# A two-layer trunk kernel: where the T2 weight sums of one feed-forward product wait for their second use, how its activations are re-read, and how its norm is computed

## The chip, the cores and the metric

The kernel runs on one core of a Trainium2 chip. The metric is the device time of one execution in microseconds. Before the change, three runs took 1405.94, 1411.48 and 1411.53 us, so the median is 1411.48.

The core has a matrix engine (TensorE, PE in the profile, with its weight loads as PEld), a vector engine (VectorE, DVE), a scalar engine (ScalarE, ACT), GpSimd (POOL) and SyncE (SP). The data is in DRAM; engines work on tiles of 128 partitions in SBUF, and TensorE accumulates in PSUM. Every transfer is a DMA that an engine's queue issues; here SyncE, ScalarE and GpSimd issue them. An engine works through its own instructions in order, so an instruction that waits holds back those behind it.

## The reference

A trunk of two layers runs over 256 context tokens and 256 latent tokens, with model width D = 1024 and FFN width F = 2816. The mixer of layer 0 is an mLSTM; that of layer 1 is multi-head latent attention (MLA). Each mixer is followed by a convolutional FFN, and each of the four sub-layers ends in the same norm:

```python
def _conv_ffn(h, w_in, conv_w, conv_b, w_out):
    gate, up = jnp.split(h @ w_in, 2, axis=-1)
    return (jax.nn.silu(_dwconv(gate, conv_w, conv_b)) * up) @ w_out
...
        f = _conv_ffn(_modulate(x, ml[3], ml[4]), ffn_w_in[i], ...)
        x = _layer_norm(ALPHA * x + ml[5] * f, ln_g[i, 1], ln_b[i, 1])
```

`_layer_norm` subtracts the mean of a row of 1024 and divides by the root of its variance plus EPS. In layer 1 the MLA first makes small projections: `w_dkv` (1024 to 256 + 64) of context and latent, `w_dq` (1024 to 384) of the latent, a norm of each, and from those `w_ukv` (keys `kn` and values) and `w_uq` (queries). Context tokens are needed in layer 1 as keys and values only.

The change concerns the second product of layer 0's FFN (activations of 512 tokens times `w_out`, 2816 x 1024), the norm behind it, and the order of MLA's projections.

## The kernel before, in words

**Arithmetic.** All is float32, computed on TensorE with operands of type fp32r split in two parts, hi and lo = value - hi. A product is three matmuls, hi x hi, hi x lo and lo x hi (L382 to L384 in `mm3`, and the loop of L1386). So each weight and each activation is split once: ScalarE casts hi, VectorE subtracts lo.

**The stream of weights.** All weights pass, in one fixed order, through the class `Stream`, in tiles of 128 x 1024 (512 KB; "raw"). `_load` (L271) takes a tile from a ring of buffers and asks for it: a plain load on SyncE (L280) or, for two sorts named below, a re-load from DRAM on SyncE (L277) followed by a GpSimd DMA that adds another weight to the tile in passing (L278). `_split` makes hi and lo (L322 ScalarE, L325 VectorE) in one of three buffers `w` (NB = 3), or, for keys marked wide, in two tiles of the pool `u` (NU = 31 tiles of 128 x 1024). `use(key)` gives the next weight to its product and splits ahead: up to AHEAD = 8 weights, as far as `limit` and the three buffers allow. A raw buffer becomes free with its split, and then the next load is asked for.

**The product of the FFN in question** (`w_fout0`, L1351) uses a scheme with seven block products where plain blocking has eight. Tokens are cut in context and latent, channels in even and odd blocks of 128, columns in halves of 512. Four sums of activations (S1 to S4) and four of weights (T1 to T4) are formed; T4 = T2 + B21. `_sum` (L291 to L293) makes T1, T2 and T3 of three raw tiles on VectorE, SUMS = 5 weights ahead. The weights come as six rounds i = 0..5 of `yt2` (T2), `y11`, `yt3`, `yt1` (24 matmuls of 128x512 each, 12 in round 5), and then in the order YLAST: `y21` of 0, 1, `yt4` of 0 to 5, `y21` of 2 to 5, `y22` of 0 to 5. T2 is used in the first part and needed again for T4 in the second: `_split` stores it to a DRAM tile `t2d` on ScalarE's queue (L324), and the load of `yt4` reads it back and has B21 added. An earlier product of the mLSTM (`vt2`, `vt4`) does the same.

Activations: `act_sums` (L1328) is called while the FFN's first product runs. It makes the operands of the first part in SBUF (`fa`, `fs`), and GpSimd stores those of the second part, named "2", "3" and "S4", to DRAM tiles `fd` (L1340, L1346). `operand()` (L1363) is called after each product from the seventh on: ScalarE's queue re-reads one operand, 128 x 512, as two DMAs of 128 KB (L1367, tile `zr`), and the operand asked for two calls before is split (L1373 ScalarE, L1374 VectorE, tile `fz`). PSUM holds four pairs of sums, p6, p1, p7, p5. Between the parts, ScalarE and VectorE form u1, u2, u3, v of them (L1420 to L1435); TensorE's next `y21` adds into p1 only when the copy of L1420 has read it.

**Rows and norm.** After 14 and 18 products GpSimd asks for the gate rows and the residual rows `z` (L1411, L1415), first latent, then context. `add()` (L1442 to L1444) multiplies the product by the gate, adds it to `z` and takes batch statistics per half row. `z_norm` (L1479) turns them into mean and variance (L1486), takes a root on ScalarE (L1488) and a reciprocal, and normalizes one half of the row on VectorE (L1492) and one on ScalarE (L1493). These pieces are Python generators in a list `bg`; `tick(n)` after a product emits n steps of them. `latent()` runs from the third `y21` on, so that its transposes `zT` (`lat_T`, L1198) fall between the last products; `context()` runs in `mla_down`.

**Layer 1's projections.** `mla_down` (L1590): `dkv` of the latent, whose three weights stay in the three `w` buffers until the context has used them too (`hold`, `unhold`); the context's adds and norm; `dq` (L384); transposes `ckT` (L1550) of the normalized rows `ckr` (L1503), and their split (L1554, L1555); the context's transposes; `ukn(1)` (latent keys); `dkv` of the context. `mla` (L1637): `uv((2,3))` (latent values), transposes `cqT` (L1649), `uqr` (qr), `ckT` of the context, `ukn(0)`, `uv((0,1))` (context keys and values), rotations, then `queries(i)` and the scores.

**Order.** The tile scheduler of the language orders instructions on each engine by its own estimate and by data; `keep_in_program_order` (`pin`) holds single instructions to the order of the program, and inside `manual_schedule` (the second part of the product and `mla_down`) TensorE's order is that of the program.

## Time and profile before

| | before |
|---|---|
| profiled execution, its own time | 1407.69 us |
| its span | 1405.8 us |
| mean granted TensorE clock | 0.992 |
| three runs | 1405.94, 1411.48, 1411.53 us |
| PE busy, 941 to 1030 us (second FFN product) | 72.67 of 89 us |
| PE busy, 1030 to 1120 us (its end, norm, projections) | 82.59 of 90 us |
| PE busy, 1120 to 1406 us | 272.39 of 286 us |

The table's last three rows are from the view that cuts the span in stretches. In the rows below, L12 is line 12 of the kernel before; "out<-in" names the tiles; "x24" is a count; `[10.90 <-ACT u L1420]` is time in which the engine waited for the instruction named. Rows of single instructions begin with the start and the duration in microseconds; where several equal ones are drawn together, the duration covers them all. PEclk is the granted clock of TensorE, 1.00 at full speed. "DMA share" is the mean busy share of the core's 16 DMA engines.

### The profile page before, as it was taken

The page shows a single profiled execution, that of the slowest core. Times are in us where ns is not written, and L with a number is a line of the kernel's source. Part 1 is how long each engine was busy: PE and PEld are TensorE (multiplying, and loading weights), DVE is VectorE, ACT ScalarE, POOL GpSimd, SP SyncE. Part 2 cuts the span into 40 slices and gives each one's busy share as a digit, 9 for nine tenths or more (in the row PEclk, how much of TensorE's full clock was granted, in tenths as well). Part 3 has the DMA queues.
Part 4 walks back from the last instruction along what each step waited for, and adds up shares of the span by engine and source line. Part 5 has one row for each costly group of instructions (what it writes and reads, how often), then busy time and mean ns, then how long its engine had stood idle before and what let it go on. Part 6 is the DMA issues. An engine that isn't in the chain of part 4 may idle for free.

```text
span 1405.8 us, 19141 instructions
## 1 busy us (share of the span) xinstructions
PE 1356.3 (96%) x6903; PEld 1141.3 (81%) x6903; DVE 1068.4 (76%) x1706; ACT 697.7 (50%) x1173; POOL 121.2 (9%) x215
## 2 busy tenths in 40 slices
PE   6999999999999999999999999999698899999997
PEld 3788888888788888878888888888477898899986
DVE  6598756687688697698799887679487788777773
ACT  6585444445544535374553433335356567455560
POOL 0032000011011001110011000000200101000000
PEclk9999999999999999999999999999899999999999
DMA  9689848779666374676857877547976325357750
GB/s 338 220 290 318 287 163 244 242 264 302 214 220 187 115 233 157 201 226 202 256 158 263 273 230 237 169 141 243 300 221 190 125 76 195 127 188 227 207 190 31
DMA packets 97903, 297.63 MB, mean 212 GB/s; under 512 B 12136, under 2 KB 24808, under 8 KB 97808
## 3 DMA queue, kind: packets, MB, share of 16 engines
q1 hardware_dynamic: 68672, 218.52, 48.4%
q0 software_dynamic: 17472, 57.57, 13.1%
q10 hardware_dynamic: 11664, 20.32, 4.0%
q8 instruction: 54, 0.88, 0.3%
q14 instruction: 41, 0.34, 0.1%
HBM read 262.90 MB, written 33.46 MB: 211 GB/s over the span
## 4 chain that ended last, share of the span: by engine, by line
PE 87%; DMA 5%; DVE 4%; ACT 2%; issue 1%; SPq 0%; ACTq 0%; DVEq 0%
PE fin L382 9%; PE fin L383 9%; PE fin L384 9%; PE tok L382 6%; PE tok L383 6%; PE tok L384 6%; PE y L1386 5%; PE qk L382 4%; PE qk L384 4%; PE qk L383 4%; PE y L383 3%; PE y L384 3%; PE y L382 3%; DMA zr<-fd 2%; PE up L382 2%; PE up L384 2%
## 5 line engine op out<-in xcount | busy, mean ns | idle before, releaser
L325 DVE TENSOR_TENSOR w<-raw,w 128x1024 fp32r<-128x1024 f32 (+1 forms) x289 | 347.8, 1206 | 181.1 <-ACT w L322 175.0
L322 ACT CAST w<-raw 128x1024 fp32r<-128x1024 f32 (+1 forms) x289 | 299.5, 1037 | 337.4 <-PE fin L384 105.2
L383 PE MATMUL fin<-h,w 128*128 128x256 f32 (+1 forms) x696 | 231.8, 333 | 0.0
L384 PE MATMUL fin<-h,w 128*128 128x256 f32 (+1 forms) x696 | 231.5, 333 | 0.0
L382 PE MATMUL fin<-h,w 128*128 128x256 f32 (+1 forms) x696 | 231.3, 333 | 0.1
L511 DVE SCALAR_TENSOR_TENSOR junk<-ar,bc 128x1024 f32<-128x1024 f32 x128 | 156.1, 1219 | 4.2 <-ACT bc L553 1.8
L383 PEld LDWEIGHTS fin<-h,w 128*128 128x128 f32 x696 | 132.2, 190 | 13.1 <-DVE h L1211 0.2
L384 PEld LDWEIGHTS fin<-h,w 128*128 128x128 f32 x696 | 132.2, 190 | 12.7
L382 PEld LDWEIGHTS fin<-h,w 128*128 128x128 f32 x696 | 131.9, 190 | 13.1 <-ACT h L1210 0.3
L382 PE MATMUL qk<-xc,w 128*128 128x512 f32 x256 | 100.7, 393 | 0.0
L384 PE MATMUL qk<-xc,w 128*128 128x512 f32 x256 | 100.0, 390 | 0.0
L383 PE MATMUL qk<-xc,w 128*128 128x512 f32 x256 | 99.8, 390 | 0.0
L1386 PE MATMUL y<-w,fz 128*128 128x512 f32 x198 | 48.6, 403 | 13.9 <-ACT u L1420 10.9
L1386 PEld LDWEIGHTS y<-w,fz 128*128 128x128 f32 x198 | 37.6, 193 | 23.6 <-ACT u L1420 11.8
L382 PEld LDWEIGHTS qk<-xc,w 128*128 128x128 f32 x256 | 48.1, 188 | 10.1 <-issue 0.4
L384 PEld LDWEIGHTS qk<-xc,w 128*128 128x128 f32 x256 | 48.1, 188 | 9.9
L383 PEld LDWEIGHTS qk<-xc,w 128*128 128x128 f32 x256 | 48.1, 188 | 9.7
L382 PE MATMUL up<-hT,w 128*128 128x512 f32 x128 | 50.5, 394 | 0.5 <-ACT hT L387 0.5
L383 PE MATMUL up<-hT,w 128*128 128x512 f32 x128 | 50.1, 392 | 0.4 <-DVE hT L388 0.4
L384 PE MATMUL up<-hT,w 128*128 128x512 f32 x128 | 50.1, 392 | 0.3 <-DVE w L388 0.3
L383 PE MATMUL tok<-w,hT 128*128 128x512 f32 x128 | 49.8, 389 | 0.0
L382 PE MATMUL tok<-w,hT 128*128 128x512 f32 x128 | 49.8, 389 | 0.0
(432 smaller groups left out, 2964.1 us busy)
## 6 DMA issues: line engine op xcount, KB each, us to landing
raw<-in_ws SPq DMA_DIRECT2D x287, 512.0 KB, 4.4
ar<-in_adaT SPq DMA_DIRECT2D x80, 512.0 KB, 4.8
adaw<-in_ada_w SPq DMA_DIRECT2D x32, 256.0 KB, 6.0
t2d<-raw ACTq DMA_DIRECT2D x13, 512.0 KB, 4.6
raw<-t2d SPq DMA_DIRECT2D x13, 512.0 KB, 7.6
raw<-in_ws POOLq DMA_DIRECT2D x13, 512.0 KB, 9.2
zr<-fd ACTq DMA_DIRECT2D x33, 128.0 KB, 5.8
xmd<-xr POOLq DMA_DIRECT2D x16, 256.0 KB, 4.7
```

The costliest lines, as they stand in the source:

```text
L322: k.nc.scalar.copy(h[:, :cols], src)
L325: k.nc.vector.tensor_sub(l[:, :cols], src, h[:, :cols])
L382: mm(out, w[0], x[0], start=start, stop=False)
L383: mm(out, w[0], x[1], start=False, stop=False)
L384: mm(out, w[1], x[0], start=False, stop=stop)
L511: nc.vector.scalar_tensor_tensor(o, w, 1.0, self.bc[j], op0=ALU.mult, op1=ALU.mult, accum_out=col[:, k, j:j + 1])
L1386: nc.tensor.matmul(ps[b], a[:, p, ts], w[q][:, cs], start=j == 0 and n == 0 and not more, stop=j == 10 and n == 2, skip_group_check=True)
```

## The change

- **T2 stays in SBUF.** For the FFN's product, T2 lives in a tile of the pool `u` (at most six). When VectorE has subtracted its lo, GpSimd adds B21 to that same tile by one DMA, and `yt4` takes it as its raw tile. The store to `t2d` and the re-load are left out (the mLSTM's product keeps them). The ring of raw buffers loses the two `u` tiles that it had in this stage.
- **Re-reads.** The DRAM tile `fd` holds two neighbouring blocks side by side, so an operand is re-read by one DMA of 256 KB instead of two of 128. `operand()` runs every other product from the twelfth on in the first part, and splits the operand asked for three calls before.
- **Rows.** The gate and `z` rows are asked for at `yt4` of round 0 (latent) and 3 (context).
- **Norm.** `add()` takes the row sum with the addition. `z_norm` gets the variance from two Squares on ScalarE with the mean as bias, and normalizes the whole row on ScalarE. The context's first two adds move to `y22` of rounds 0 and 1, and two steps are emitted after each later `y22`.
- **Splitting ahead.** The `dkv` weights are wide (tiles of `u`, not the three `w` buffers). `limit` is set to the projections' keys at the start of the product, and to the fourth weight of the product before the FFN's first one. The sums of weights are bounded by `limit` too.
- **Order of projections.** `uv((2,3))` moves ahead of `dkv` of the context; `ukn(0)` and `uv((0,1))` move behind `queries(0)` and `queries(1)`.

```diff
@@ -111 +111 @@
-        add(("dkv", 0, c), m * 320)
+        add(("dkv", 0, c), m * 320, True)
@@ -251 +251 @@
-                          [("ar", 2)] * 2 + [("u", NU)] * 2))
+                          [("ar", 2)] * 2))
@@ -255,2 +255,11 @@
-    def ring(self, j):
-        return [x for x in self.bufs if x[0] <= j][-1]
+        self.y0 = keys.index(("yt2", 0, 0))
+        self.slot, self.t2 = [], {}
+        n = {}
+        for j, key in enumerate(keys):
+            j0, ring = [x for x in self.bufs if x[0] <= j][-1]
+            if key[0] in ("yt2", "yt4"):
+                self.slot.append(("t2", NU, 6))
+                continue
+            tag, bufs = ring[n.get(j0, 0) % len(ring)]
+            n[j0] = n.get(j0, 0) + 1
+            self.slot.append((tag, bufs, [x[0] for x in ring].count(tag)))
@@ -265,3 +274,5 @@
-        j0, ring = self.ring(self.nl)
-        tag = ring[(self.nl - j0) % len(ring)][0]
-        return [self.tags[j] for j in self.raw].count(tag) < [x[0] for x in ring].count(tag)
+        key = self.order[self.nl][0]
+        if key[0] == "yt2" and key[2] and self.nu < self.y0 + 4 * max(key[2] - 2, 0):
+            return False
+        tag, _, n = self.slot[self.nl]
+        return [self.tags[j] for j in self.raw].count(tag) < n
@@ -273,5 +284,7 @@
-        j0, ring = self.ring(j)
-        tag, bufs = ring[(j - j0) % len(ring)]
-        t = k.pool.tile([128, CW], F32, tag=tag, name="raw", bufs=bufs)
-        if key[0] in ("vt4", "yt4"):
-            k.nc.sync.dma_start(t[:, :cols], k.t2d[key[0][0], key[1], key[2]][:, :cols])
+        tag, bufs, _ = self.slot[j]
+        if key[0] == "yt4":
+            t = self.t2.pop(key)
+        else:
+            t = k.pool.tile([128, CW], F32, tag="u" if tag == "t2" else tag, name="raw", bufs=bufs)
+        if key[0] == "vt4":
+            k.nc.sync.dma_start(t[:, :cols], k.t2d[key[1], key[2]][:, :cols])
@@ -279 +292 @@
-        elif key[0] not in ("vt2", "yt2"):
+        elif key[0] not in ("vt2", "yt2", "yt4"):
@@ -302 +315 @@
-        while self.nsum < min(j + SUMS, self.n):
+        while self.nsum < min(j + SUMS, max(self.limit, j + 1)):
@@ -323,2 +336,2 @@
-            if key[0] in ("vt2", "yt2"):
-                k.nc.scalar.dma_start(k.t2d[key[0][0], key[1], key[2]][:, :cols], src)
+            if key[0] == "vt2":
+                k.nc.scalar.dma_start(k.t2d[key[1], key[2]][:, :cols], src)
@@ -325,0 +339,4 @@
+            if key[0] == "yt2":
+                t4 = ("yt4",) + key[1:]
+                k.nc.gpsimd.dma_start(src, self.ws[self.ids[t4][0], :, :cols], accum_op=ALU.add)
+                self.t2[t4] = raw
@@ -589,2 +606 @@
-        self.t2d = {(n, p, j): self.dr.tile([128, 1024], F32, name="t2d")
-                    for n, a, b in (("v", 2, 4), ("y", 1, 6)) for p in range(a) for j in range(b)}
+        self.t2d = {(p, j): self.dr.tile([128, 1024], F32, name="t2d") for p in range(2) for j in range(4)}
@@ -1336 +1352,3 @@
-        d = self.dr.tile([128, 768], F32, name="fd")
+        if j % 2 == 0:
+            self.fd.append(self.dr.tile([128, 3, 512], F32, name="fd"))
+        d = self.fd[-1][:, :, j % 2 * 256:j % 2 * 256 + 256]
@@ -1340 +1358 @@
-        nc.gpsimd.dma_start(d[:, 0:512], x2)
+        nc.gpsimd.dma_start(d[:, 0:2], x2.rearrange("p (x n) -> p x n", x=2))
@@ -1346 +1364 @@
-        nc.gpsimd.dma_start(d[:, 512:768], x1[:, a])
+        nc.gpsimd.dma_start(d[:, 2], x1[:, a])
@@ -1349 +1366,0 @@
-        self.fd.append(d)
@@ -1358 +1375 @@
-        off = {"2": 0, "3": 256, "S4": 512}
+        off = {"2": 0, "3": 1, "S4": 2}
@@ -1366,2 +1383,2 @@
-                for h, j in enumerate(js):
-                    pin(nc.scalar.dma_start(r[:, h * 256:(h + 1) * 256], self.fd[j][:, off[x]:off[x] + 256]))
+                n = 256 * len(js)
+                pin(nc.scalar.dma_start(r[:, :n], self.fd[i][:, off[x], :n]))
@@ -1369 +1386 @@
-            if len(got) > 2 or not parts and got:
+            if len(got) > 3 or not parts and got:
@@ -1391,0 +1409,2 @@
+        st.limit = kv0
@@ -1396 +1415 @@
-        z, gate = [None] * 4, []
+        z, gate = [None] * 4, [None, None]
@@ -1406 +1425 @@
-                if n >= 6:
+                if n >= 11 and n % 2:
@@ -1408,8 +1426,0 @@
-                if n in (14, 18):
-                    g = 1 - len(gate)
-                    r = self.uf("gate")
-                    nc.gpsimd.dma_start(r, self.gd[0, 5][1 - g:2 - g, :].to_broadcast([128, 1024]))
-                    gate.append(r)
-                    for b in range(2):
-                        z[2 * g + b] = self.uf("z")
-                        nc.gpsimd.dma_start(z[2 * g + b], x1d[2 * g + b])
@@ -1431,2 +1442 @@
-        gate = gate[::-1]
-        stats = [self.tiny(12, "st").rearrange("p (a b) -> p a b", b=6) for _ in range(4)]
+        sums = [self.tiny(4, "zs") for _ in range(4)]
@@ -1437,0 +1448,8 @@
+        def rows(g):
+            r = self.uf("gate")
+            nc.gpsimd.dma_start(r, self.gd[0, 5][1 - g:2 - g, :].to_broadcast([128, 1024]))
+            gate[g] = r
+            for b in range(2):
+                z[2 * g + b] = self.uf("z")
+                nc.gpsimd.dma_start(z[2 * g + b], x1d[2 * g + b])
@@ -1438,0 +1457 @@
+            i = c.start // 512
@@ -1443,2 +1462,2 @@
-                nc.vector.tensor_tensor(zz, zz, r, op=ALU.add)
-                nc.vector.bn_stats(stats[2 * g + b][:, c.start // 512], zz)
+                nc.vector.scalar_tensor_tensor(zz, zz, 1.0, r, op0=ALU.mult, op1=ALU.add,
+                                               accum_out=sums[2 * g + b][:, i:i + 1])
@@ -1449 +1468 @@
-            for _ in self.z_norm(z[2:4], stats[2:4]):
+            for _ in self.z_norm(z[2:4], sums[2:4]):
@@ -1457 +1476 @@
-            yield from self.z_norm(z[0:2], stats[0:2])
+            yield from self.z_norm(z[0:2], sums[0:2])
@@ -1459 +1477,0 @@
-        st.limit = kv0
@@ -1468 +1486,3 @@
-                if (name, i) == ("yt4", 0):
+                if name == "yt4" and i in (0, 3):
+                    rows(1 if i == 0 else 0)
+                if (name, i) == ("yt4", 3):
@@ -1472 +1492,3 @@
-                self.tick(1)
+                if name == "y22" and i < 2:
+                    next(low)
+                self.tick(2 if name == "y22" and i else 1)
@@ -1475 +1497 @@
-                    self.bg.append(add(0, lo, p1))
+                    low = add(0, lo, p1)
@@ -1481 +1503 @@
-    def z_norm(self, zs, stats):
+    def z_norm(self, zs, sums):
@@ -1484,10 +1506,13 @@
-        for z, st in zip(zs, stats):
-            mv = self.tiny(2, "mv")
-            nc.vector.bn_aggr(mv, st)
-            rs = self.tiny(1, "rs")
-            nc.scalar.activation(rs, mv[:, 1:2], AF.Sqrt, bias=self.keps, scale=1.0)
-            nc.vector.reciprocal(rs, rs)
-            nm = self.tiny(1, "nm")
-            nc.vector.scalar_tensor_tensor(nm, mv[:, 0:1], -1.0, rs, op0=ALU.mult, op1=ALU.mult)
-            nc.vector.tensor_scalar(z[:, 0:512], z[:, 0:512], mv[:, 0:1], rs, op0=ALU.subtract, op1=ALU.mult)
-            nc.scalar.activation(z[:, 512:1024], z[:, 512:1024], AF.Identity, bias=nm, scale=rs)
+        for z, v in zip(zs, sums):
+            nc.vector.tensor_tensor(v[:, 0:1], v[:, 0:1], v[:, 1:2], op=ALU.add)
+            nc.vector.tensor_scalar(v[:, 0:1], v[:, 0:1], -1.0 / D, None, op0=ALU.mult)
+            for h in range(2):
+                jk = self.s2("jk")
+                nc.scalar.activation(jk, z[:, h * 512:(h + 1) * 512], AF.Square, bias=v[:, 0:1], scale=1.0,
+                                     accum_out=v[:, 2 + h:3 + h])
+            yield
+            nc.vector.tensor_tensor(v[:, 2:3], v[:, 2:3], v[:, 3:4], op=ALU.add)
+            nc.scalar.activation(v[:, 2:3], v[:, 2:3], AF.Sqrt, bias=self.keps, scale=1.0 / D)
+            nc.vector.reciprocal(v[:, 2:3], v[:, 2:3])
+            nc.vector.tensor_tensor(v[:, 0:1], v[:, 0:1], v[:, 2:3], op=ALU.mult)
+            nc.scalar.activation(z, z, AF.Identity, bias=v[:, 0:1], scale=v[:, 2:3])
@@ -1625,0 +1651 @@
+        self.uv((2, 3))
@@ -1641 +1666,0 @@
-        self.uv((2, 3))
@@ -1665,3 +1689,0 @@
-        self.ukn(0)
-        self.uv((0, 1))
-        self.ckT = self.wk = self.wv = None
@@ -1763 +1784,0 @@
-        Ps, PTs = {}, {}
@@ -1765,0 +1787,4 @@
+        Ps, PTs = {}, {}
+        self.ukn(0)
+        self.uv((0, 1))
+        self.ckT = self.wk = self.wv = None
@@ -1865,0 +1891 @@
+        st.limit = st.y0 + 4
```

## The prediction

> **What bounds the kernel now.** I read the page's shares first, then a table by stretch, then the waits of the stretch the change touches, then single instructions.
>
> ```profile
> PE 1356.3 (96%) x6903; PEld 1141.3 (81%) x6903; DVE 1068.4 (76%) x1706; ACT 697.7 (50%) x1173; POOL 121.2 (9%) x215
> ```
> ```profile
> core 0: us, PE busy (x) PEld busy (x) DVE busy (x) ACT busy (x) POOL busy (x), PEclk, DMA share, GB/s
> 1005.00:1035.00 30.00, 16.66 (x62) 12.44 (x63) 17.58 (x25) 12.55 (x19) 1.96 (x3) 0.83 0.92 277
> 1035.00:1067.00 32.00, 32.00 (x149) 26.50 (x148) 22.88 (x36) 18.56 (x27) 0.00 (x0) 1.00 0.56 169
> 1067.00:1100.00 33.00, 26.84 (x173) 25.80 (x172) 31.38 (x72) 21.93 (x51) 2.20 (x4) 0.90 0.63 196
> ```
> TensorE is busy 96% of the span, so a change that leaves its 6903 matmuls alone can win only where TensorE waits. The widest hole is 1005 to 1035 (16.66 busy of 30, clock 0.83, DMA engines 92% busy); a smaller one follows at 1067 to 1100. Both lie in the stretch that is edited. What ends the waits there (engine, line, releaser: total, times, longest):
>
> ```profile
> PE y L1386 <- ACT u L1420: 10.9, 1, 10.9
> PE ckT L1550 <- DVE ckr L1503: 5.8, 2, 4.8
> PE y L1386 <- DVE w L325: 2.6, 2, 2.3
> PE y L1386 <- ACT w L322: 2.5, 2, 1.6
> PE kn L383 <- DVE ckT L1555: 2.3, 1, 2.3
> PE kn L382 <- ACT ckT L1554: 0.9, 1, 0.9
> PE qr L382 <- ACT cqT L1649: 0.4, 1, 0.4
> ```
> ScalarE's queue just before the 10.9:
>
> ```profile
> 1007.02 1.04 ACT L322 CAST w<-raw 128x1024 fp32r<-128x1024 f32 x1 [4.25 <-DMA zr<-fd]
> ...
> 1014.23 0.62 ACT L1373 CAST fz<-zr 128x512 fp32r<-128x512 f32 x1 [5.34 <-DMA zr<-fd]
> ...
> 1014.75 0.58 ACT L1420 COPY u<-y 128x512 f32<-128x512 f32 x1
> ```
> The copy that frees TensorE's accumulator (L1420) is ready at 1004 but stands in ScalarE's queue behind two casts that wait for re-read activations (zr). Those land late because the queues carry this, all at once (last two numbers: KB each, median us to landing):
>
> ```profile
> zr<-fd ACTq DMA_DIRECT2D x33, 128.0 KB, 5.8
> raw<-t2d SPq DMA_DIRECT2D x5, 512.0 KB, 10.6
> raw<-in_ws POOLq DMA_DIRECT2D x5, 512.0 KB, 14.4
> z<-x1d POOLq DMA_DIRECT2D x4, 512.0 KB, 14.0
> ```
> ```profile
> DMA to landing us min/median/max: 2.5/5.8/19.3
> ```
> The last row is zr's alone: worst 19.3 us.
>
> **Term A: the holes up to the first transposes.**
>
> ```profile
> L1386 PE MATMUL y<-w,fs x132: 388/389/499, 941.4 to 1004.1; 128*128 128x512 f32 x132
> ```
> ```profile
> 976.78 5.60 PE L1386 MATMUL y<-w,fa 128*128 128x512 f32 x24
> 982.22 5.60 PE L1386 MATMUL y<-w,fs 128*128 128x512 f32 x24
> ...
> 1015.38 7.41 PE L1386 MATMUL y<-w,fz 128*128 128x512 f32 x24 [10.90 <-ACT u L1420]
> ```
> ```profile
> 1053.66 0.60 PE L1198 MATMUL zT<-ident,z 128*128 128x128 f32 x4
> ```
> 24 matmuls start every 5.44 us, 0.2267 each. From 941.4 to the first zT at 1053.66 are 112.3 us, and 132+132+144 = 408 matmuls need 92.5. So 19.8 us are lost: 16.0 in the L1386 waits above, 1.8 in the slow 24 after the long one, the rest in pieces.
>
> What the change does to it: six stores of T2 (ScalarE's queue) and six reloads (SyncE's) go, about 5.8 MB both ways; B21 is added by the same six GpSimd requests, issued as soon as VectorE has subtracted, at least 21 us before use (the last one: from step yt2 of round 5 to the cast of its yt4, eight steps), so their 14.4 us are covered (without that cover each excess microsecond would hold the cast, and TensorE). The 33 re-reads of 128 KB become 18, asked for three operands ahead of their cast where it was two. ScalarE issues 15+6 DMAs fewer ahead of its casts; SyncE's weight loads no longer queue behind reloads that wait for buffers. The rest of the loss goes if the re-reads land within their slack. That slack, from the built order: a re-read is cast three steps after its request (8.2 us at 2.72 a step), and the weight cast queued behind it has another 3, so 11 us against a median of 5.8 and a worst of 19.3.
>
> A new wait stands at the first zT. The norm of the latent rows must fit between the last yt4 product and that transpose. VectorE's rows first: they start 0.59 apart behind a 512-column operation and 1.14 behind a weight's subtraction.
>
> ```profile
> 1035.57 0.68 DVE L1443 TENSOR_TENSOR z<-z,zp 128x512 f32<-128x512 f32 x1
> 1036.16 1.22 DVE L325 TENSOR_TENSOR w<-raw,w 128x1024 fp32r<-128x1024 f32 x1
> 1037.30 0.69 DVE L1444 BATCH_NORM_STATS2 st<-z 128x6 f32<-128x512 f32 x1
> ...
> 1040.94 0.69 DVE L1442 TENSOR_TENSOR zp<-y,gate 128x512 f32<-128x512 f32 x1 [1.09 <-PE y L1386]
> ```
> ```profile
> 1048.12 1.28 ACT L1488 ACT_TABLE_LOAD   x1
> 1049.42 0.30 ACT L1488 ACTIVATE rs<-mv,keps 128x1 f32<-128x1 f32 x1
> ...
> 1052.62 0.81 ACT L1493 ACTIVATE z<-z,nm,rs 128x512 f32<-128x512 f32 x1
> ```
> ```profile
> 476.15 0.62 ACT L1102 ACTIVATE jk<-oh 128x512 f32<-128x512 f32 x1
> 476.67 0.19 ACT L1102 ACTIVATION_READ_ACCUMULATOR jk<-oh 128x1 f32 x1
> ...
> 477.43 0.19 ACT L1102 ACTIVATION_READ_ACCUMULATOR jk<-oh 128x1 f32 x1
> ```
> ```profile
> L553 ACT ACTIVATE bc<-bc x4: 1059/1062/1077, 67.8 to 371.7; 128x1024 f32<-128x1024 f32 x4
> ```
> Before, 12.7 us lie between (1040.94 to 1053.66) and the norm ends at 1053.43, 0.2 ahead. After, VectorE reaches the row sums at 6.6 us (two products and two adds 2.4, two and a half weights 2.9, one and a half operands 0.9, tiny ops 0.4); the batch statistics (four of 0.6) and the half normalized on VectorE (two of 0.5) are gone. ScalarE then has four Squares with their reads (0.76 apiece, the distance of two such pairs), the table load 1.28, two roots 0.6, a weight cast 1.0 and two whole-row writes of 1.06: 8.0. So the rows are ready at about 14.6, 2.0 late. Bounds: 0 (sums earlier) and 4 (two casts more between the steps).
>
> What else is late next: behind the end of y11 in round 5 VectorE has, in one row, adds (L1422, L1428), subtractions (L1435) and weights. The first weight starts when its cast is done, at 1.65, and then follow weight, three adds, weight, two subtractions, an operand and the third weight: 1.65 + 3x1.14 + 6x0.59 = 8.6, wanted by TensorE at two short steps, two long ones and two matmuls: 2.7 + 5.4 + 0.5 = 8.6. I take 0.5 (bounds 0 and the 2.3 of the old L325 wait). Term A: -19.8 + 0.5 + 2.0 = **-17.3**.
>
> **Term B: the latent and context projections.**
>
> ```profile
> 1083.61 0.34 PE L384 MATMUL dq<-wu,hl 128*128 128x384 f32 x1
> 1088.78 0.47 PE L1550 MATMUL ckT<-ident,ckr 128*128 128x128 f32 x1 [4.83 <-DVE ckr L1503]
> 1090.20 1.33 PE L1550 MATMUL ckT<-ident,ckr 128*128 128x128 f32 x5 [0.94 <-DVE ckr L1503]
> 1091.32 3.18 PE L1198 MATMUL zT<-ident,z 128*128 128x128 f32 x16
> ```
> TensorE is done at 1083.9 and waits 5.8 for ckr, which stands in VectorE's queue (31.38 busy of 33) behind the context's gated sums and the split weights. Between 1040.94 and 1090.2, 49.3 us, VectorE loses about 6.8 us (eight statistics, four halves) and gains 3.5 (five and two half operands, now cast later), 2.9 (uqr and uqn weights, split here because the dkv weights no longer hold the three w buffers) and 1.2 of tiny ops: level. ScalarE gains 6.1 (eight Squares), 1.0 (four whole rows at 1.06 for halves at 0.81), 3.7 (the operands at 0.62 or half) and 2.6 (the weights at 1.04 or half), 13.4 in all, on 40.5 busy of 65 (two rows of the table); it has room but stands in the chain before each root. So this chain hardly shortens: I take 48.3 for 49.3, **-1.0**. Bounds: -5.8 (the wait gone) and +3 (a quarter of ScalarE's extra work in the chain). Moving two of four gated sums ahead of the end of y22 is what pays for the later operands.
>
> **Term C: queries and keys.**
>
> The waits at qr and kn (0.4, 0.9, 2.3) stand in the table above. uv((2,3)), 24 matmuls, moves ahead of dkv on the context; ukn(0) and uv((0,1)) move behind 36 query matmuls of 256 columns (half of 0.2267, about 4.1 us). They cover the 3.2 us at kn; but the rms of ckr now stands on ScalarE between dkv and cqT (two squares of half the width and two roots, about 1.5 us) without uv's 5.4 us as cover, so the wait at qr grows from 0.4 to about 1.4. Net -2.2, taken as **-2.0** (bounds -3.5 and +1).
>
> Everything else hides: the 11 GpSimd stores of two parts at once, now in rows of 1 KB, have no reader for at least a round (without that the re-reads behind them would be late by the excess); the new limit on splitting ahead leaves three w buffers full as before; the row loads (gate, z) wait in the built order for products of the first three rounds alone and go out after the last B21 request, some 19 us before use against 14.0.
>
> **Sum.** -17.3 - 1.0 - 2.0 = -20.3 on the profiled execution's own 1407.69 (span 1405.8): 1387.4. The three runs average 1409.65, 1.96 above it, and their median is 1411.48; I forecast **1389**.
>
> A page's rule that would shift this: the row first, 24 matmuls took 7.41 instead of 5.60 after the 10.90 wait, and 16 transposes 3.18 after the 4.83 one, where four took 0.60 at 1053.66. The Trainium skill, "TensorE: Matmul & The Clock Gate", Part 1, says that the array's clock halves after an idle window of about 3.4 us. By it the waits that I leave in term B, about 2.4 and 2.0, would be too short to slow anything, and the sum would be some 0.8 lower (3.18 less four times 0.60), 1388.2; the rows show slow stretches behind 4.83 and 10.90 and none for a wait of that size quoted here, so I keep it.
>
> **Rivals.**
> Half the gain (0.20): the six row loads, 3.1 MB, now leave together behind the last B21 request, just where eight re-reads are asked for. One re-read at the worst 19.3 has 8 us more than its slack of 11, and TensorE waits that long: 1397. For it: DMA 92% busy at 1005 to 1035. Against: 5.8 MB fewer and twice the row length.
> The engines become the bound (0.10): TensorE's earlier end is given back because VectorE and ScalarE keep their pace from the last yt4 on, B at its +3, the zT wait at 4, C at +1: 1389 + 4 + 2 + 3 = 1398.
> It doesn't do what it says (0.06): re-reads are late for another reason than the T2 traffic (the weights alone), the 10.9 stays in ScalarE's queue and only the small waits go: 1405 to 1411.
> Slower (0.06): VectorE halts at the first gated sum (L1442's place) for the row loads, as every weight subtraction is queued behind it. They have 19 us of cover; from 48 us to landing on, over three times the 14.0 shown, it would eat all 20 and 9 more: 1418.6 or above.
>
> **How the numbers follow.** My forecast has 0.58, 1382 to 1393 from A, B and C within half of their bounds. The range 1381 to 1401 adds both middle rivals and leaves the last two outside. A change below 0.5% (7 us) can hardly be told from none here. Faster by more than that, below 1404.4: 0.58+0.20+0.10 = 0.88; within: 0.06; slower: 0.06.
>
> **What would show it.** Right: no t2d row between 941 and 1030; zr x18 of 256 KB; no L1420-like wait over 1 us; a new wait of about 2 at the first zT; ckT waits of 4 to 5 in all; none at kn. Wrong: ScalarE waiting for zr with TensorE behind it, or VectorE waiting for gate or z.

## The result

The changed kernel takes 1386.99 us (median of four runs, 1385.21 to 1388.08), the kernel before 1409.83 beside it (1405.94 to 1411.53): a ratio of 0.9841, 95% interval 0.9815 to 0.9866. The forecast was 1389. The profiled execution took 1388.08 us with a span of 1386.3, 19.5 less than before.

(One figure of the description above needs mending: a product of the scheme has 12 matmuls, 6 in round 5. A row with x24 is two products drawn together.)

The shares of busy time, and all that TensorE waited for between 930 and 1150 us:

```profile
PE 1356.3 (98%) x6903; PEld 1143.7 (83%) x6903; DVE 1061.5 (77%) x1710; ACT 705.3 (51%) x1189; POOL 122.5 (9%) x215
```
```profile
PE ckT L1575 <- DVE ckr L1528: 4.8, 2, 3.0
PE zT L1214 <- ACT z L1518: 1.9, 1, 1.9
PE qr L399 <- ACT cqT L1674: 0.6, 1, 0.6
```

TensorE does the same 1356.3 us of work; only its waits changed. The 16 us of waits inside the FFN's product and the 3.2 at kn are gone, ckT keeps 4.8 of 5.8, and a new wait of 1.9 stands at the first zT. TensorE's rows around that new wait, and the table by stretch with the granted clock:

```profile
1001.56 32.91 PE L1403 MATMUL y<-w,fz 128*128 128x512 f32 x144
1034.39 0.33 PE L1214 MATMUL zT<-ident,z 128*128 128x128 f32 x1
1036.65 0.55 PE L1214 MATMUL zT<-ident,z 128*128 128x128 f32 x3 [1.94 <-ACT z L1518]
1036.95 4.58 PE L1403 MATMUL y<-w,fz 128*128 128x512 f32 x12
...
1041.73 3.00 PE L1403 MATMUL y<-w,fz 128*128 128x512 f32 x12
```
```profile
core 0: us, PE busy (x) PEld busy (x) DVE busy (x) ACT busy (x) POOL busy (x), PEclk, DMA share, GB/s
1030.00:1034.00 4.00, 4.00 (x19) 3.33 (x18) 0.73 (x5) 3.97 (x9) 0.00 (x0) 1.00 0.44 139
1037.00:1040.00 3.00, 3.00 (x10) 2.32 (x9) 2.97 (x6) 3.00 (x6) 0.00 (x0) 0.52 0.29 112
1042.00:1046.00 4.00, 4.00 (x21) 3.28 (x21) 3.81 (x8) 3.68 (x9) 0.00 (x0) 1.00 0.48 157
```

From the first fz product on, 144 matmuls run without a hole. Behind the 1.94 wait the granted clock is 0.52 for 3 us, and 12 matmuls take 4.58 us where the next 12 take 3.00. To see where the time went, three points of TensorE's work are compared: the first dkv of the latent, the first kn, the first score s. Before, then after (count, ns minimum/median/maximum, first and last start):

```profile
L382 PE MATMUL dkv<-w,hl x16: 308/309/392, 1067.7 to 1075.0; 128*128 128x320 f32 x16
L382 PE MATMUL kn<-ckT,wu x32: 277/283/385, 1094.3 to 1127.8; 128*128 128x256 f32 x32
L382 PE MATMUL s<-kn,qn x16: 388/398/478, 1138.3 to 1174.2; 128*128 128x512 f32 x16
```
```profile
L1403 PE MATMUL y<-w,fs x132: 389/389/389, 941.7 to 1001.3; 128*128 128x512 f32 x132
L399 PE MATMUL dkv<-wu,hl x16: 305/309/309, 1052.4 to 1059.0; 128*128 128x320 f32 x16
L399 PE MATMUL kn<-ckT,wu x32: 278/283/562, 1077.5 to 1112.1; 128*128 128x256 f32 x32
L399 PE MATMUL s<-kn,qn x16: 389/398/486, 1118.3 to 1154.3; 128*128 128x512 f32 x16
```

The product starts at 941.4 before and 941.7 after. From there to dkv: 126.3 to 110.7 us, so -15.6. From dkv to kn: 26.6 to 25.1, -1.5. From kn to s: 44.0 to 40.8, -3.2. From s to the end of the span: 267.5 to 268.0, +0.5. With 0.3 from the later start these make the 19.5 (1405.8 less 1386.3).

The re-reads' issues in the stretch and their times to landing (minimum, median, maximum), after:

```profile
zr<-fd ACTq DMA_DIRECT2D x15, 256.0 KB, 3.2
...
z<-x1d POOLq DMA_DIRECT2D x4, 512.0 KB, 14.3
```
```profile
DMA to landing us min/median/max: 2.0/3.0/7.0
```

The worst re-read fell from 19.3 to 7.0 us. Which part of the change did that is what the experiments had to say.

### The profile page after: what moved, and what is told of

Its sections match the earlier page's. It is cut to its first block, busy times and chain, and to the rows that moved or that the text cites. A ratio compares the mean times of both kernels' runs of the same rounds, so it can differ in the third digit from the quotient of the medians.

```text
span 1386.3 us, 19100 instructions
## 1 busy us (share of the span) xinstructions
PE 1356.3 (98%) x6903; PEld 1143.7 (83%) x6903; DVE 1061.5 (77%) x1710; ACT 705.3 (51%) x1189; POOL 122.5 (9%) x215
## 4 chain that ended last, share of the span: by engine, by line
PE 91%; ACT 3%; DVE 3%; DMA 2%; issue 1%; SPq 0%; DVEq 0%; ACTq 0%
PE fin L399 9%; PE fin L400 9%; PE fin L401 9%; PE y L1403 7%; PE tok L399 6%; PE tok L401 6%; PE tok L400 6%; PE qk L399 4%; PE qk L401 4%; PE qk L400 4%; PE y L400 3%; PE y L401 3%; PE y L399 3%; PE up L399 2%; PE up L400 2%; PE up L401 2%
## 5 line engine op out<-in xcount | busy, mean ns | idle before, releaser
L338 DVE TENSOR_TENSOR w<-raw,w 128x1024 fp32r<-128x1024 f32 x286 | 344.1, 1206 | 165.0 <-ACT w L335 164.2
L335 ACT CAST w<-raw 128x1024 fp32r<-128x1024 f32 x286 | 297.0, 1039 | 326.7 <-PE fin L401 100.8
L338 DVE TENSOR_TENSOR wu<-raw,wu 128x1024 fp32r<-128x1024 f32 (+3 forms) x37 | 43.0, 1177 | 10.2 <-ACT wu L335 10.0
L399 PE MATMUL tok<-w,hT 128*128 128x512 f32 x128 | 49.8, 389 | 0.0
L400 PE MATMUL tok<-w,hT 128*128 128x512 f32 x128 | 49.8, 389 | 0.0
L401 PE MATMUL tok<-w,hT 128*128 128x512 f32 x128 | 49.8, 389 | 0.0
```

The source lines that it names most:

```text
L335: k.nc.scalar.copy(h[:, :cols], src)
L338: k.nc.vector.tensor_sub(l[:, :cols], src, h[:, :cols])
L399: mm(out, w[0], x[0], start=start, stop=False)
L400: mm(out, w[0], x[1], start=False, stop=False)
L401: mm(out, w[1], x[0], start=False, stop=stop)
```

## The experiments

Each was timed beside the kernel before on the same chip, and is compared with the changed kernel by the ratios: 0.9841 for it; 0.001 is 1.4 us. The interval of that 0.9841 is wide and overlaps with those of some of its variants that are called slower below. The single times do not overlap: each run of these variants took 1389.26 us or more, and no run of the changed kernel over 1388.08.

**Single parts on the kernel before.** First T2 in SBUF alone (the new loading and splitting of yt2 and yt4, without the other parts):

```diff
+            if key[0] == "yt2":
+                t4 = ("yt4",) + key[1:]
+                k.nc.gpsimd.dma_start(src, self.ws[self.ids[t4][0], :, :cols], accum_op=ALU.add)
+                self.t2[t4] = raw
```

> The kernel before with one part of the change: T2 of the FFN's product stays in SBUF and has B21 added there (ring of raw buffers without the two u tiles); re-reads of 128 KB, norm, rows and order of projections as before. Theory (the 10.9 us wait at the copy of L1420 and the waits for weights come from the 5.8 MB of T2 stores and re-loads that share the queues with the re-reads): the L1386 waits fall from 16 us to 4 or less, time 12 to 16 us under before, so 1394 to 1398. Rival A (the 33 re-reads of 128 KB themselves, issued in small pieces just in time, are late): 0 to 4 us under before, 1406 to 1410. Rival B (the rows gate and z, 3.1 MB asked for after products 14 and 18, crowd the re-reads): 0 to 4 us under before.

Measured: 1400.04 us against 1410.42, ratio 0.9925 (0.9908 to 0.9941), 10.4 us. Then the re-reads alone:

```diff
-                for h, j in enumerate(js):
-                    pin(nc.scalar.dma_start(r[:, h * 256:(h + 1) * 256], self.fd[j][:, off[x]:off[x] + 256]))
+                n = 256 * len(js)
+                pin(nc.scalar.dma_start(r[:, :n], self.fd[i][:, off[x], :n]))
```

> The kernel before with one part of the change: the re-reads as 18 DMAs (256 KB, three of 128 KB) from the paired layout, at the old pace; T2 through DRAM as before. Theory: the queues stay crowded by T2, the worst re-read falls somewhat below 19.3 us and the 10.9 us wait to some 6 to 8; 3 to 5 us under before, 1405 to 1407. Rival A: the L1386 waits fall to 4 us or less, 1394 to 1398. Rival B: no change, 1408 to 1411.

Measured: 1403.70, ratio 0.9948 (0.9931 to 0.9965), 6.7 us. TensorE's longest wait, 10.9 at the copy of u before, is now:

```profile
PE y L1387 <- ACT u L1421: 6.8, 1, 6.8
```

Then both:

> The kernel before with both of the parts above. Theory: L1386 waits under 2 us, no wait at the first zT (the old norm is kept), waits at ckT as before: 16 to 19 us under before, 1391 to 1394. Rival A: the same as with the re-reads alone, 1394 to 1398. Rival B (rows still asked for early): still 10 us of waits, 1400 or more.

Measured: 1396.91, ratio 0.9901 (0.9886 to 0.9915), 13.5 us, less than the 17.1 that the two gave singly. What TensorE still waited for in the product with T2 in SBUF alone, and how its re-reads landed:

```profile
PE y L1402 <- ACT w L335: 5.6, 2, 4.3
```
```profile
DMA to landing us min/median/max: 2.2/6.0/10.7
```

With the T2 traffic away the worst re-read still takes 10.7 us, and two weight casts still stand behind re-reads. Each part alone lands between the theory and rival A, and both together in A's range: neither cause alone carries the 16 us. T2 in SBUF is worth 10.4 us with small pieces and 6.8 with 256 KB pieces (1403.70 to 1396.91), both at the old pace.

**T2 undone in the changed kernel.** Back to a DRAM tile, six stores on ScalarE's queue and six re-loads on SyncE's:

```diff
-        if key[0] == "yt4":
-            t = self.t2.pop(key)
...
-        if key[0] == "vt4":
+        if key[0] in ("vt4", "yt4"):
...
-            if key[0] == "yt2":
-                t4 = ("yt4",) + key[1:]
-                k.nc.gpsimd.dma_start(src, self.ws[self.ids[t4][0], :, :cols], accum_op=ALU.add)
```

> The changed kernel with one part undone: T2 goes to DRAM and back (six stores on ScalarE's queue, six re-loads on SyncE's queue), all else changed. Theory: 8 to 13 us above the changed kernel, 1395 to 1400, with waits for weights and re-reads at L1403. Rival A and B (the re-reads in 256 KB pieces, or the rows asked for later, are what mattered): within 3 us of the changed kernel, 1385 to 1390.

Measured: 1387.59, ratio 0.9838 (0.9824 to 0.9853): nothing lost. The theory as it stood falls. TensorE's waits in the product, and the re-reads' landing:

```profile
PE y L1397 <- DVE w L335: 0.5, 1, 0.5
PE y L1397 <- ACT w L332: 0.3, 1, 0.3
```
```profile
DMA to landing us min/median/max: 4.5/7.8/10.3
```

The queues are as crowded as the prediction feared: the re-reads take 7.8 us in the median, more than the 5.8 of the kernel before. They do no harm: 10.3 is still inside the 11 us between request and need that the prediction estimated for the new pace, and ScalarE's casts of re-read data hardly wait any more. Their waits between 985 and 1035 us, in the kernel before and here:

```profile
ACT fz L1373 <- DMA zr<-fd: 12.5, 5, 5.3
```
```profile
ACT fz L1384 <- DMA zr<-fd: 0.3, 1, 0.3
```

That suggested the pace as the cause, so it was tried alone on the kernel before and undone in the changed one:

```diff
-                if n >= 6:
+                if n >= 11 and n % 2:
...
-            if len(got) > 2 or not parts and got:
+            if len(got) > 3 or not parts and got:
```

> The kernel before with one part of the change: operands are asked for after every other product from the twelfth on (before: after every product from the seventh on), and split three requests later (before: two). 128 KB pieces, T2 through DRAM, rows, norm and order of projections as before. Since undoing T2 in the changed kernel cost nothing, theory 2: the time between a re-read's request and its cast is what mattered, and the burst of 18 requests within 18 products. It expects most of the L1386 waits (16 us) to go: 10 to 16 us under before, 1394 to 1400. Rival (rows gate and z asked for early are what crowds the queues): under 4 us, 1406 to 1411.

Measured: 1403.79, ratio 0.9953 (0.9939 to 0.9968), 6.2 us; its ten runs spread from 1398.66 to 1408.36. That is above the rival's 4 and well short of the theory's 10 to 16: with T2 through DRAM and small pieces the worst re-read still takes 16.1 us there, and the new pace alone does not cover it.

> The changed kernel with the old pace of re-reads alone (a request after every product from the seventh on, split two requests later), T2 in SBUF and 256 KB pieces kept. Theory 2: waits for re-reads return, as in the kernel before with T2 in SBUF and 256 KB pieces (3.2 us before L1403 there): 2 to 5 us above the changed kernel, 1389 to 1392. Rival (rows): no change, 1386 to 1388.

Measured: 1392.26, ratio 0.9879 (0.9864 to 0.9894), 5.4 us lost, a little more than the theory's 2 to 5. TensorE waits again in the product, ScalarE waits again for re-reads, and their landing:

```profile
PE y L1403 <- DVE w L338: 3.6, 3, 2.3
```
```profile
ACT fz L1390 <- DMA zr<-fd: 6.7, 5, 2.7
```
```profile
DMA to landing us min/median/max: 3.0/6.0/10.4
```

They land no later than in the run with T2 in DRAM (median 7.8, worst 10.3). What was in time at the new pace is late at the old one.

Third, the pieces: two DMAs of 128 KB for each operand in the changed kernel.

```diff
-                pin(nc.scalar.dma_start(r[:, :n], self.fd[i][:, off[x], :n]))
+                for h in range(len(js)):
+                    c = slice(h * 256, h * 256 + 256)
+                    pin(nc.scalar.dma_start(r[:, c], self.fd[i][:, off[x], c]))
```

> The changed kernel with each operand re-read as two DMAs of 128 KB (33 instead of 18); pace and T2 in SBUF kept. The runs so far: each of T2 in SBUF, 256 KB pieces and the new pace gains 6 to 10 us alone, two of them together nearly everything (pace and 256 KB pieces without T2 in SBUF: nothing lost). Theory 3 (the three are substitutes: each gives a re-read more time than it needs) expects this pair, pace and T2 in SBUF, to lose nothing as well: within 1.5 us of the changed kernel, 1385.5 to 1388.5. Rival (the pieces are what the pace needs): 3 to 7 us above it.

Measured: 1392.88, ratio 0.9894 (0.9865 to 0.9923), 7.5 us lost by the ratios and 5.9 by the medians. By time theory 3 falls in its simple form: the pieces matter too, T2 does not. But it is not the re-reads that are late here: they land within 8.0 us, and no wait of a cast is put down to them. The loss is not at the product, where only 1.2 us of waits appear, but at the transposes behind it, where 1.9 became 4.6:

```profile
PE zT L1214 <- ACT z L1520: 4.6, 2, 2.6
PE y L1405 <- DVE w L338: 1.2, 1, 1.2
```

The norm starts late. ScalarE's first Square in this run, and behind it, in a fence of its own, that of the changed kernel:

```profile
1014.31 1.05 ACT L335 CAST w<-raw 128x1024 fp32r<-128x1024 f32 x1 [3.30 <-DMA raw<-in_ws]
...
1032.67 1.05 ACT L335 CAST w<-raw 128x1024 fp32r<-128x1024 f32 x1 [1.67 <-PE y L1405]
1033.63 0.72 ACT L1513 ACTIVATE jk<-z,zs 128x512 f32<-128x512 f32 x1
```
```profile
1027.71 1.05 ACT L335 CAST w<-raw 128x1024 fp32r<-128x1024 f32 x1 [1.58 <-PE y L1403]
1028.66 0.72 ACT L1511 ACTIVATE jk<-z,zs 128x512 f32<-128x512 f32 x1
```

The Squares begin 5.0 us later. In both kernels they stand behind a cast that waits until TensorE has freed a weight buffer. In the built order of this run that is one weight cast further on (the 14th from 999 us on, the 13th in the changed kernel), and ScalarE had lost time earlier (3.3 us for a weight, in the row shown). How much comes from the 15 more requests and how much from the scheduler's other order was not separated.

The three parts side by side: what ScalarE's casts of re-read data waited for them (the view of the tile zr), and all that TensorE waited in the product, in us.

| run | T2 | pieces | pace | ScalarE for re-reads | TensorE in the product |
|---|---|---|---|---|---|
| before | DRAM | 128 KB | old | 12.5 | 16.4 |
| T2 alone | SBUF | 128 KB | old | 11.9 | 5.6 |
| pieces alone | DRAM | 256 KB | old | 15.0 | 9.4 |
| pace alone | DRAM | 128 KB | new | 6.2 | 4.6 |
| T2 and pieces | SBUF | 256 KB | old | 8.3 | 3.2 |
| changed, old pace | SBUF | 256 KB | old | 6.9 | 3.6 |
| changed, small pieces | SBUF | 128 KB | new | 0.0 | 1.2 |
| changed, T2 in DRAM | DRAM | 256 KB | new | 0.3 | 0.8 |
| changed | SBUF | 256 KB | new | 2.0 | 0.0 |

At the old pace the casts wait for 6.9 us or more, whatever the rest; at the new pace with either of the other two parts, 2.0 or less. So the pace is what the re-reads need, and it needs one of the other two beside it. (The last four rows have the other parts of the change too.)

**Where the rows are asked for.** The calls for gate and z go back to where n is 14 and 18; n counts from 0, so that is behind the 15th and 19th product:

```diff
-                if name == "yt4" and i in (0, 3):
-                    rows(1 if i == 0 else 0)
...
+                if n in (14, 18):
+                    rows(1 if n == 14 else 0)
```

> The changed kernel with the gate and residual rows asked for where they were before, after products 14 and 18 of the first part. Theory 2: the six row loads hold u tiles earlier but the re-reads keep their slack: within 1.5 us of the changed kernel. Rival (rows asked for early crowd re-reads and weights): 4 to 10 us above it, 1391 to 1397.

Measured: 1386.80, ratio 0.9842 (0.9825 to 0.9859). Their place is worth nothing that can be measured, and the rival that made them the crowd falls.

**The order of the projections** put back:

```diff
         self.ukn(1)
-        self.uv((2, 3))
         rows = self.dkv_mm(hc, wd)
...
         queries(0)
         queries(1)
-        self.ukn(0)
-        self.uv((0, 1))
```

> The changed kernel with the old order of projections: uv((2,3)) after dkv of the context, ukn(0) and uv((0,1)) ahead of the queries. Term C of the prediction expects the waits at kn (3.2 us) back and the wait at qr down from 0.6 to 0.4: 2 to 3.5 us above the changed kernel, 1389 to 1390.5. Rival (the waits at kn came from VectorE and ScalarE being behind, which the wide dkv weights have mended): within 1 us of it.

Measured: 1391.61, ratio 0.9872 (0.9858 to 0.9887), 4.4 us lost, more than the theory's 2 to 3.5; the rival, a loss within 1 us, falls. TensorE's waits at kn are back, 2.3 and 0.9, and the table by stretch (columns as above) shows the clock low behind them:

```profile
1104.00:1107.00 3.00, 1.47 (x7) 1.47 (x8) 3.00 (x7) 0.00 (x0) 1.62 (x3) 0.71 0.91 356
```

The slow matmuls are not the old ones. The kernel before has the same two waits, and behind them kn at full speed. Its rows, then those of this run:

```profile
1119.78 0.62 PE L382 MATMUL kn<-ckT,wu 128*128 128x256 f32 x3 [0.85 <-ACT ckT L1554]
1122.67 0.39 PE L383 MATMUL kn<-ckT,wu 128*128 128x256 f32 x1 [2.27 <-DVE ckT L1555]
1122.89 0.28 PE L384 MATMUL kn<-ckT,wu 128*128 128x256 f32 x1
```
```profile
1102.63 0.61 PE L399 MATMUL kn<-ckT,wu 128*128 128x256 f32 x3 [0.85 <-ACT ckT L1579]
1105.53 0.58 PE L400 MATMUL kn<-ckT,wu 128*128 128x256 f32 x1 [2.28 <-DVE ckT L1580]
1105.91 0.41 PE L401 MATMUL kn<-ckT,wu 128*128 128x256 f32 x1
```

Behind the matmul that waited 2.28 or 2.27 us, the next 14 start within 3.15 us here and within 1.77 before. So undoing the order costs the 3.2 us of waits and about 1.4 of slow matmuls, less the 0.2 that the wait at qr gets back: 4.4 in all.

**The norm.** Old statistics and half rows, at the new places:

```diff
-                nc.vector.scalar_tensor_tensor(zz, zz, 1.0, r, op0=ALU.mult, op1=ALU.add,
-                                               accum_out=sums[2 * g + b][:, i:i + 1])
+                nc.vector.tensor_tensor(zz, zz, r, op=ALU.add)
+                nc.vector.bn_stats(sums[2 * g + b][:, i], zz)
```

> The changed kernel with the old norm (batch statistics on VectorE, half of each row normalized on either engine), at the places of the new one. The prediction's working: VectorE gets eight statistics of 0.6 and four halves of 0.5 back, ScalarE loses eight Squares of 0.76. In the latent's chain this takes the wait at the first zT (1.9 us, and 1.7 us of half clock behind it) to between 0 and 2; the context's chain stays within 1 us: 0 to 4 us below the changed kernel, 1383 to 1387. Rival (VectorE is the tighter engine there, so the move to ScalarE is what keeps the ckT wait at 4.8): 2 to 5 us above it, 1389 to 1392.

Measured: 1385.45, ratio 0.9834 (0.9808 to 0.9860). The medians are 1.5 us apart and the intervals overlap, so by time alone it is no worse; the rival's loss of 2 to 5 us is not there. The time lies in the theory's range, but not for its reason: it expected the wait at the first zT to shrink and the context's chain to stay. The trace shows two opposite effects, in TensorE's waits and in its first 12 matmuls behind the waited zT:

```profile
PE zT L1214 <- DVE z L1515: 2.8, 2, 2.0
PE ckT L1573 <- DVE ckr L1526: 2.4, 2, 1.4
```
```profile
1037.93 5.47 PE L1403 MATMUL y<-w,fz 128*128 128x512 f32 x12
```

The latent's rows come later (2.8 us of waits for 1.9, and 12 matmuls in 5.47 for 4.58), the wait at ckT halves. So a further run takes the new norm for the latent and the old one for the context:

```diff
-            yield from self.z_norm(z[0:2], sums[0:2])
+            yield from self.z_norm_bn(z[0:2], sums[0:2])
```

> The changed kernel with the new norm for the latent's rows and the old one for the context's rows. With the old norm for both, the first zT ended 1.0 us later than with the new one and 12 matmuls behind it took 5.47 us instead of 4.58, while dkv to kn took 21.9 us instead of 25.1. Theory (in the latent's chain VectorE is the tighter engine, so Squares on ScalarE help; in the context's chain ScalarE is, so they hurt): dkv of the latent starts as in the changed kernel, 110.6 us after the product's start, and kn follows 22 to 24 us behind: 1 to 3 us below the changed kernel, 1384 to 1386, and no worse than the old norm for both (1385.45). Rival (the shorter stretch from dkv to kn was only the later start of dkv, with ckr ready at a fixed time): same as the changed kernel, 1386.5 to 1387.5.

Measured: 1385.16 (five runs, 1383.89 to 1386.98), ratio 0.9823 (0.9805 to 0.9841). TensorE's waits, and its dkv and kn:

```profile
PE ckT L1597 <- DVE ckr L1550: 3.0, 2, 1.9
PE zT L1214 <- ACT z L1523: 1.9, 1, 1.9
```
```profile
L399 PE MATMUL dkv<-wu,hl x16: 305/309/309, 1052.9 to 1059.5; 128*128 128x320 f32 x16
L399 PE MATMUL kn<-ckT,wu x32: 278/283/363, 1075.6 to 1110.0; 128*128 128x256 f32 x32
```

The product starts at 942.2 there: dkv 110.7 us behind it, as in the changed kernel, and kn 22.7 us behind dkv where it was 25.1. The trace gives the theory its 2.4 us, and speaks against the rival, as dkv starts no later; the times (0.9823 against 0.9841) agree but do not prove it, their intervals overlap.

**Two moves against the waits that are left.** One more step ahead of the latent's transposes, and the rms of ckr ahead of the context's norm:

```diff
             yield
             yield
+            yield
             yield from lat_T(z[2:4])
...
+        rows = self.dkv_rows(rows, 2)
         for _ in context:
             pass
-        rows = self.dkv_rows(rows, 2)
```

> The changed kernel with two moves: the transposes of the latent rows start one step later (12 matmuls, 2.72 us, go ahead of them), and the rms of the latent's ckr is emitted ahead of the context's norm. Theory (TensorE waits 1.9 us for the last row write and 4.8 us for ckr, and runs at half clock for some 3 us behind each): the first wait and its slow 1.7 us go, and of the second some 2 to 4 us; 4 to 7 us below the changed kernel, 1380 to 1383. Rival (the context's rows come later by what ckr takes, and the wait moves from ckT to the transposes behind it): 2 to 4 us below it, all from the first move, 1383 to 1385.

Measured: 1390.57, ratio 0.9871 (0.9842 to 0.9899), 4.2 us lost; both theory and rival had a gain. TensorE's waits:

```profile
PE zT L1214 <- ACT z L1519: 7.1, 2, 5.7
PE y L1403 <- ACT w L335: 1.0, 1, 1.0
PE y L1403 <- DVE w L338: 0.5, 1, 0.5
...
PE ckT L1576 <- DVE ckr L1564: 0.4, 1, 0.4
```

The rival's mechanism is the right one, and stronger than it said. ckT is down from 4.8 to 0.4, but the context's rows, now behind ckr, hold the transposes for 7.1. At the first zT the wait moved into the product as 1.5 us on the weight casts.

## Why the prediction was right, point by point

The sum, -20.3, met a measured -19.5 in the profiled span, and -22.8 in the medians (the profiled run is the slowest of the four). That it came so close is in part luck: term A gave 1.7 us less than forecast, B and C together 1.7 more, and 0.8 went outside the three terms. The terms:

**Term A**, -17.3: from the product's start to the first zT were 112.3 us before (1053.66 - 941.4), and to the zT behind the new wait 94.9 after (1036.65 - 941.7), -17.4. Its pieces were off in both directions. The 0.5 at the turn between the two parts didn't come: there is no wait in the 144 matmuls. The new wait at the first zT was forecast at 2.0 and is 1.9, but in this trace it also costs 1.6 us of half clock (4.58 for 3.00), so that term A is -15.6 at dkv.

The step that named the cause failed. It gave the removed T2 traffic as what goes, and the slack of the re-reads as a condition. The runs turn this round: without T2 in SBUF, but with the new pace and 256 KB pieces, nothing is lost; with the old pace 5.4 us are, with small pieces 5.9 to 7.5. T2 in SBUF is worth 10.4 us where pace and pieces are old, 6.8 where the pace alone is old, and nothing where both are new. The slack was the right thing to compare a landing with: at the new pace's 11 us a worst of 10.3 did no harm, and at the old pace, with a step of 2.72 less and so an estimated 8, a worst of 10.4 did.

**Term B**, -1.0: -1.5. ckT waits 4.8, inside the 4 to 5 that was to be seen. That ScalarE stands in the chain is what the old norm for the context shows: with it, ckT waits 3.0. That VectorE comes out level was not shown by itself.

**Term C**, -2.0: -3.2, and 4.4 when undone. The mechanism was right, the size too small: the waits at kn went, and qr grew by 0.2 us where 1.0 was taken. The slow matmuls that make it 4.4 when undone are no part of the -3.2, as the kernel before has none there.

**The rule that would have shifted the sum.** The rows showed slow stretches behind 4.83 and 10.90 only, and by the rule waits of about 2 us would slow nothing. Here the clock falls to 0.52 behind a wait of 1.94 and to 0.71 behind 0.9 and 2.3. The Trainium skill, "TensorE: Matmul & The Clock Gate", Part 1: The HAM clock gate, gives an idle window of about 3.4 us; these waits are shorter, and the measurement decides. The same page of the Trainium skill, Part 4: PE-mode transpose, says that transposes do not count as busy in the same way; without them TensorE's gap at the first zT is 2.56 us (1034.39 to 1036.95), still less. (That the kernel's transposes run in the mode of which the page speaks is not shown here.) Nor does every such wait slow what follows: the kernel before ran 106 matmuls in 24.33 us, at full speed, behind a wait of 2.29, and full speed behind its two at kn; with the rows asked for earlier the wait at the first zT, 1.93 there, was followed by 12 matmuls in 3.01. Keeping the sum was right here, as the granted clock was 0.50 from 1075 to 1078 us, behind ckT's two waits; but no run shows when a wait of 2 us slows and when not.

**The rivals.** The row loads did take their time (z 14.3 us), but no re-read took over 7.0, and their place is worth nothing. The engines did become the bound where the second rival put them (zT, ckT), at 1.9 and 4.8, not at the ends it needed. VectorE never stood still for gate or z. The third rival was half right: the T2 traffic was not what had to go. Its time did not come, because pace and pieces mended the lateness.

What stays open: the wide dkv weights and the limits on splitting ahead were not tried alone. By an estimate there is little left for them: T2 and pieces on the kernel before (13.5), the pace and the order as lost when undone (5.4, 4.4) make 23.3 of the 22.8. The loss with small pieces is traced to the late Squares, not split further.

## What to carry to other kernels

When a queue of casts waits for re-read data, compare the landing time with the time between request and use before counting bytes: asking one request earlier and in fewer pieces made 5.8 MB of traffic free here. Parts of a change that mend the same wait are substitutes, so each must be undone in the final kernel as well as tried alone; their single gains (10.4, 6.7, 6.2) add up to 23.3 us, more than the 15.6 won up to dkv. Where a norm can run on either of two engines, decide it for each place by the engine that is ahead in the chain there.

## What was not expected of the hardware

A wait of TensorE of about 2 us can cost nearly its own length again, or nothing. In the changed kernel the one of 1.94 us was followed by 3 us at a granted clock of 0.52, 1.6 us lost; with the rows asked for earlier the same wait, 1.93, cost nothing behind it. The same two waits at kn cost 1.4 us more with the old order in the changed kernel, and nothing in the kernel before. So a difference of 1 to 2 us between two traces can be this alone.

The kernel before varies by 5.6 us between runs, with the new pace alone by 9.7, and the changed kernel by 2.9. The times go with the mean granted clock: with the new pace alone, 1398.66 us at 0.995 and 1408.36 at 0.988. Re-reads that land close to their limit, and waits that now and then halve the clock, would both give this; neither was tested by itself.
